# A hybrid encoder layer: two sets of input gates moved into a stage of seven block products ahead of the mLSTM

## The chip, the cores and the metric

The kernel runs on one core of a Trainium2 chip. The metric is the device time of one execution in microseconds (us). Several executions are timed and their median is given; one execution is recorded by the hardware profiler and is the source of every row shown.

## The reference, cut to what matters

One encoder layer is applied to two request groups with shared weights. A group is 512 tokens of 1024 features.

```python
h = rmsnorm(x, g_mix)
u = h @ w_in                       # one input projection, columns split into:
qk, v, o, gates, c_q, c_kv, k_r, gm = split(u)
# (A) bidirectional mLSTM, 4 heads, qk width 128, v width 256
qk = silu(centred_conv(qk, conv_w))                     # 5 taps along the tokens
hm = mlstm_chunkwise(q, k, v, log_i, log_f)             # both directions, added
hm = rmsnorm(hm, g_mhead)                               # per head
y_m = (sigmoid(o) * hm) @ w_mo                          # o: 1024 output gates
# (B) latent attention, 8 heads, latents of 256
y_a = mla_attention(...) @ w_ao
g_m, g_a = split(sigmoid(gm))                           # 2 x 1024 merge gates
x = x + (g_m * y_m + g_a * y_a) @ w_out
x = x + (silu(h2 @ w_gate) * (h2 @ w_up)) @ w_down      # h2 = rmsnorm(x, g_ffn), width 2816
x = x + sigmoid(x @ w_ple_gate) * (p_l @ w_ple)
return rmsnorm(x, g_final)
```

The change concerns `o` (1024 columns), part of `gm` (2048 columns) and the first rmsnorm. Everything is float32.

## The kernel before

**Layout.** Activations lie transposed: 128 features on the partitions, the 512 tokens of one group along the free dimension. The input x of a group is therefore 8 blocks of 128x512 (index `k`), for groups `g` = 0 and 1.

**Split products.** TensorE multiplies in a reduced type (fp32r in the profile). Each float32 operand is split into a high part (a cast on ScalarE) and a low part (a subtraction on VectorE, `lo_of`, L152), and a product is three matmuls: high weight by high row, high by low, low by high. One column block (128 output columns) of the input projection for one group is then 8 blocks x 3 = 24 matmuls of 128x512. This is `proj1` (L181 to L183); its weights are 512 KB, loaded on SyncE's queue and split as `whi`, `wlo` (`weight`, L166 and L152).

**Rows.** The rows that enter the input projection are x times the gain g_mix, split (`split_x`, tiles hh and hl). They are not divided by their root mean square. `norm_x` works out that factor per token, `rs1`, and spreads it over all partitions (ssc: sums over the features; rbc: spreading, by matmuls with a diagonal). `hproj` multiplies each column block by `rs1` on VectorE when it leaves PSUM (L329); for v the factor is a per-partition scale instead (L502, L503).

**mLSTM.** A head stage prepares the gate columns, the latents cq0, cq1, ckv0, ckv1, and the gate logs: the gates go to DRAM (gsd, rid) and come back in another layout (lf), pass through log-sigmoid, cumulative sums and running maxima (L378 to L443) with a trip through DRAM (lfd) for the flipped direction, and end in `nmr`, from which each chain builds its weights. Then `mlstm_proj(hd)` does the projections of a head: q and k with the convolution (VectorE, L477), v (matmuls of 128x256, L495 to L497), the scores sT, and last the two output-gate columns of the head (`to`: L329, then tanh and a scaling by hg, on ScalarE). `mlstm_chain(hd, g)` follows for each group: per direction, bc and bd (matmuls with `nmr`, L543 to L546) give the exponents, ScalarE takes exp into a tile `w` (L558; there is one), VectorE multiplies by the scores, `w` is split into ph and pl (L567, L152), and nm (L580) multiplies by v. The result is normed (ssm, L598), transposed by TensorE (ht, L602), multiplied by `to` and stored (hz). In program order the projections of head hd+1 follow the chains of head hd. Ahead of the chain of (head 3, group 0) stands `lat_norms` (constant `LATN`): it norms the latents with ssc, eight diag, rbc and eight scalings (L620 to L629). Its rbc uses the two PSUM banks (tag bc) that bc and bd use.

**Merge gates.** `merge_gate` does one of the 16 merge-gate columns for both groups by `proj1` (48 matmuls), takes the tanh and stores it to DRAM (tmd, tad). They do not depend on the mLSTM or on attention. The list `BULK` says how many stand where: 10 after the program text of the mLSTM, then 2 and the rest between the attention heads.

**Order.** Each engine works through its own queue in order. The order of the queues comes from a scheduler that simulates the program: it starts from the program's order and lets instructions pass one another where pools of tiles (`Slots`) and PSUM banks (`Banks`) allow it. Merge gates that stand behind the mLSTM in the text therefore run between the last head's matmuls.

**Seven block products.** The output projections of the two branches and the FFN use a scheme with fewer products, the class `Seven` with `Ops` (operands), `chain` (order) and `outputs`: two column blocks, two halves of the contraction and the two groups make a product of 2x2 blocks, which is done by 7 block products (P1, P2, P7, P6, P5, Q4, P3) instead of 8, each 4 x 3 = 12 matmuls (L894 to L896, tile names b, xh, xl, wp). Sums of row blocks (VectorE or GpSimd) and of weight blocks (GpSimd, L869 to L879) are built before; weights of a pair of columns come in 1 MB on ScalarE's DMA queue, and each product's weights are split when they are due.

Of the kernel before, what the change touches and what calls it, by code (L numbers as in the profile page):

```python
# [7 lines left out]
F32 = mybir.dt.float32  # L8
# [54 lines left out]
def encoder_kernel(ctx: ExitStack, tc: tile.TileContext, a):  # L63
# [67 lines left out]

    banks("P1", dict(mm=2, sc=2, tp=2, bc=2), mm="mm", sc="sT nm", tp="ssc tpc vtp ht", bc="bc bd rbc")
# [147 lines left out]

    LAT = Slots("LAT", "right", raw=8)
    H = Slots("H", h=32, rs=2)
    MC = Slots("MC", sel=2)
    X0 = Slots("X0", x=16, raw=2, tr=15)
    R = Slots("R", "right", r=12, tr=2)
    h, rs1 = [], []
    xs = [[X0("x", "x") for _ in range(KD)] for _ in range(G)]
# [16 lines left out]

# [5 lines left out]
    def raw(bk, sl=LAT):  # L310
        t = sl("raw", "raw")
        S.copy(t, bk)
        return t
# [3 lines left out]
    early["gate", 0] = raw(proj1(wg, h[0]), X0)  # L317
# [5 lines left out]
    early["gate", 1] = raw(proj1(wg, h[1]), X0)  # L323
    early["cq0", 1] = raw(proj1(wq, h[1]))
    norm_x(0)
    norm_x(1)

    def hproj(w, g, out, bk=None):
        V.tensor_tensor(out=out, in0=rs1[g], in1=proj1(w, h[g]) if bk is None else bk, op=ALU.mult)  # L329
        return out  # L330
# [14 lines left out]
    for n in ("cq1", "ckv0", "ckv1"):  # L345
        w = w8(n)
        for g in range(G):
            early[n, g] = raw(proj1(w, h[g]))
    X0.close()
# [112 lines left out]
    def mlstm_proj(hd):  # L462
        qk = [[None, None] for _ in range(G)]
        for qi, nme in enumerate(["q", "k"]):
            w = w8(f"{nme}{hd}")
            ch = 4 * qi + hd
            for g in range(G):
                bk = hproj(w, g, M1("tr", "cu"))
# [14 lines left out]
        for g in range(G):  # L483
# [14 lines left out]
            for i in range(NB):  # L498
                src = bks[i // 2][:, 256 * (i % 2) : 256 * (i % 2) + 256]
                hi_, lo_ = (v2[n][:, i, 0:256] for n in range(2))  # L500
                sc = rcol[g][:, 2 * i : 2 * i + 1]
                S.activation(out=hi_, in_=src, func=AF.Copy, scale=sc)  # L502
                V.scalar_tensor_tensor(  # L503
                    out=lo_, in0=src, scalar=sc, in1=hi_.bitcast(F32), op0=ALU.mult, op1=ALU.subtract
                )
# [16 lines left out]
        for c in range(2):  # L522
            w = w8(f"o{2 * hd + c}")
            for g in range(G):
# [114 lines left out]
    tmd = [[dr.tile([P, T], F32, name=f"tmd{g}_{c}") for c in range(KD)] for g in range(G)]  # L639
    tad = [[dr.tile([P, T], F32, name=f"tad{g}_{c}") for c in range(KD)] for g in range(G)]  # L640

    def merge_gate(name, dst, c):
        w = w8(f"{name}{c}")
        for g in range(G):
            t = hproj(w, g, EV("bk", "tg"))
            S.activation(out=t, in_=t, func=AF.Tanh, scale=0.5)
            nc.sync.dma_start(dst[g][c], t)

    bulk = [(n, d, c) for c in range(KD) for n, d in (("gm", tmd), ("ga", tad))]
# [127 lines left out]

    late = {}  # L780
    NAMES = ("P1", "P2", "P7", "P6", "P5", "Q4", "P3")

    def op(name, n, dt):
        return (H if name in ("P1", "P2", "P7", "P6") else late["OP"])("h", n, dt)

    class Ops:

        def __init__(self, raw, tmp, sums):  # L790
            self.raw, self.tmp, self.sums = raw, tmp, sums
            self.r, self.t, self.x = {}, {}, {}

        def get(self, n, k):
            if (n, k) not in self.r:
                self.r[n, k] = self.raw({"a": 0, "b": 1, "c": 0, "d": 1}[n], k + 4 * (n in "cd"))
            return self.r[n, k]

        def part(self, name, k):
            if name in ("P1", "P2", "P3"):  # L800
                return self.get({"P1": "a", "P2": "c", "P3": "d"}[name], k)
            add = self.sums(name).tensor_tensor
            if name == "P7":
                t = self.t[k] = self.tmp() or self.get("b", k)
                add(out=t, in0=self.get("b", k), in1=self.get("d", k), op=ALU.subtract)
            elif name == "P6":
                t = self.t[k]
                add(out=t, in0=t, in1=self.get("a", k), op=ALU.subtract)
            elif name == "P5":
                t = self.get("a", k)  # L810
# [29 lines left out]
    def wsplit(src):  # L840
        n, t = src.shape[-1], wpair()
        hi, lo = t[:, 0:n], t[:, n : 2 * n]
        S.copy(hi, src)  # L843
        lo_of(lo, src, hi)
        return hi, lo

    class Seven:


# [583 lines left out]
```

## Time and profile before

| | |
|---|---|
| median of 3 runs | 1907.61 us (1904.54 to 1908.16) |
| the profiled execution | 1907.19 us |
| its span in the profile | 1905.4 us |
| mean granted TensorE clock | 0.988 |
| TensorE busy | 1849.6 us, 97% |
| VectorE busy | 1242.5 us, 65% |
| ScalarE busy | 879.7 us, 46% |
| GpSimd busy | 477.5 us, 25% |
| DMA | 207.58 MB, mean 109 GB/s |

In the rows, PE is TensorE (PEld its weight loads, beside PE), DVE VectorE, ACT ScalarE, POOL GpSimd, SP SyncE. A row of the time order gives the start, the duration, engine, source line, operation, output <- inputs with their sizes, how many were joined (x8), and in brackets the idle time before with what ended it. Matmuls overlap in the pipeline: a matmul's duration is longer than the distance from its start to the next one's.

### The profile page before, as it was taken

Reading aid. Unit: us, or ns where it says so; the run is one execution under the profiler, and the core shown is the slowest. Engines: PE = TensorE matmul, PEld = TensorE weight load, DVE = VectorE, ACT = ScalarE, POOL = GpSimd, SP = SyncE. Lnnn points to the kernel's source line nnn. Section 1 sums busy time; section 2 is a strip of 40 time slices with the busy share of each in tenths; the row PEclk is TensorE's granted clock in tenths of the full one; section 3 lists DMA queues with packets and bytes.
Section 4 is the critical chain, followed back from the end, with each engine's and each line's share of the span. In section 5 each row is a group of like instructions: output and inputs, shape, how many; then the busy total and the mean of one; then the engine's idle time right before and its main releaser. Section 6 shows DMA issues by size and latency. Waiting matters only on the chain.

```text
span 1905.4 us, 24519 instructions
## 1 busy us (share of the span) xinstructions
PE 1849.6 (97%) x8840; PEld 1538.6 (81%) x8840; DVE 1242.5 (65%) x2141; ACT 879.7 (46%) x1711; POOL 477.5 (25%) x346
## 2 busy tenths in 40 slices
PE   7999999999999999899989998999999999999997
PEld 6898998988888878677877886888888887888886
DVE  7657575836556567976897577444444558878757
ACT  5255555644444565784434354333333344434442
POOL 3000000100000000342550026666465652322100
PEclk9999999999999999999999998999999999999999
DMA  4111111122253123345455241233222346534242
GB/s 164 51 45 34 56 34 56 34 67 73 78 176 132 54 70 110 106 149 210 154 184 181 88 166 50 100 112 109 94 100 93 129 137 222 162 130 141 89 127 89
DMA packets 97881, 207.58 MB, mean 109 GB/s; under 512 B 10656, under 2 KB 21280, under 8 KB 97760
## 3 DMA queue, kind: packets, MB, share of 16 engines
q1 hardware_dynamic: 85664, 163.03, 25.5%
q10 hardware_dynamic: 12096, 43.00, 7.0%
q8 instruction: 69, 1.13, 0.2%
q14 instruction: 52, 0.43, 0.1%
HBM read 151.89 MB, written 54.10 MB: 108 GB/s over the span
## 4 chain that ended last, share of the span: by engine, by line
PE 85%; DVE 8%; issue 2%; ACT 2%; POOL 1%; DMA 1%; SPq 0%; DVEq 0%; ACTq 0%; POOLq 0%
PE b L894 12%; PE b L896 12%; PE b L895 12%; PE mm L183 8%; PE mm L181 8%; PE mm L182 8%; PE nm L580 3%; DVE xl L152 2%; PE mm L79 2%; PE mm L495 2%; PE mm L497 2%; PE mm L496 2%; PE pt L759 1%; DVE wp L152 1%; PE mm L1243 1%
## 5 line engine op out<-in xcount | busy, mean ns | idle before, releaser
L894 PE MATMUL b<-xh,wp 128*128 128x512 f32 x1148 | 444.1, 395 | 13.3 <-ACT wp L843 6.4
L895 PE MATMUL b<-xl,wp 128*128 128x512 f32 x1148 | 451.1, 393 | 4.9 <-DVE xl L152 4.9
L896 PE MATMUL b<-xh,wp 128*128 128x512 f32 x1148 | 447.2, 394 | 3.7 <-DVE wp L152 3.6
L843 ACT CAST wp<-wst 128x512 fp32r<-128x512 f32 (+1 forms) x271 | 164.7, 612 | 306.7 <-PE b L896 238.8
L152 DVE TENSOR_TENSOR wp<-wst,wp 128x512 fp32r<-128x512 f32 (+1 forms) x271 | 248.3, 918 | 76.7 <-ACT wp L843 76.1
L894 PEld LDWEIGHTS b<-xh,wp 128*128 128x128 f32 x1148 | 217.4, 189 | 66.4 <-ACT wp L843 8.8
L896 PEld LDWEIGHTS b<-xh,wp 128*128 128x128 f32 x1148 | 217.4, 189 | 53.5 <-DVE wp L152 6.0
L895 PEld LDWEIGHTS b<-xl,wp 128*128 128x128 f32 x1148 | 217.4, 189 | 52.1 <-DVE xl L152 5.3
L181 PE MATMUL mm<-hh,whi 128*128 128x512 f32 x592 | 233.7, 395 | 7.4 <-ACT whi L166 7.2
L183 PE MATMUL mm<-hh,wlo 128*128 128x512 f32 x592 | 233.1, 396 | 2.3 <-DVE wlo L152 2.2
L182 PE MATMUL mm<-hl,whi 128*128 128x512 f32 x592 | 233.4, 395 | 0.7 <-DVE hl L277 0.7
L869 POOL TENSOR_TENSOR s<-wst,wst 128x512 f32<-128x512 f32 (+1 forms) x42 | 75.6, 1800 | 432.8 <-DMA wst<-w 255.0
L934 DVE TENSOR_TENSOR u<-b,u 128x512 f32<-128x512 f32 x90 | 61.6, 689 | 141.4 <-PE b L896 85.3
L181 PEld LDWEIGHTS mm<-hh,whi 128*128 128x128 f32 x592 | 112.6, 190 | 31.2 <-ACT whi L166 7.2
L183 PEld LDWEIGHTS mm<-hh,wlo 128*128 128x128 f32 x592 | 112.4, 190 | 26.6 <-DVE wlo L152 3.4
L182 PEld LDWEIGHTS mm<-hl,whi 128*128 128x128 f32 x592 | 112.4, 190 | 24.5 <-DVE hl L277 1.3
L166 ACT CAST whi<-wst 128x1024 fp32r<-128x1024 f32 (+1 forms) x71 | 73.0, 1029 | 103.9 <-PE mm L182 63.4
L152 DVE TENSOR_TENSOR xl<-ld,xh 128x512 fp32r<-128x512 f32 x121 | 97.7, 837 | 11.6 <-ACT xh L1178 6.6
L152 DVE TENSOR_TENSOR wlo<-wst,whi 128x1024 fp32r<-128x1024 f32 (+1 forms) x71 | 86.7, 1221 | 25.1 <-ACT whi L166 24.8
L929 ACT COPY u<-b 128x512 f32<-128x512 f32 x90 | 50.9, 588 | 110.6 <-PE b L896 79.1
L152 POOL TENSOR_TENSOR vnl<-avt,vnh 128x512 fp32r<-128x512 f32 x16 | 21.4, 1337 | 283.6 <-ACT vnh L156 260.9
L495 PE MATMUL mm<-whi,hh 128*128 128x256 f32 x256 | 72.3, 283 | 0.2 <-DVE cu L329 0.2
(333 smaller groups left out, 3570.4 us busy)
## 6 DMA issues: line engine op xcount, KB each, us to landing
wst<-w SPq DMA_DIRECT2D x75, 512.0 KB
wst<-w ACTq DMA_DIRECT2D x60, 512.0 KB
ld<-actd SPq DMA_DIRECT2D x77, 256.0 KB
actd<-t SPq DMA_DIRECT2D x44, 256.0 KB
actd<-sg SPq DMA_DIRECT2D x33, 256.0 KB
x<-x SPq DMA_DIRECT2D x32, 256.0 KB
ld<-hzd SPq DMA_DIRECT2D x32, 256.0 KB
wst<-wd ACTq DMA_DIRECT2D x16, 512.0 KB
```

Of the source, the lines that this page charges most:

```text
L152: e.tensor_tensor(out=out, in0=src, in1=hi.bitcast(F32), op=ALU.subtract)
L166: S.copy(hi[:, :n], st[:, :n])
L181: E.matmul(bk, whi[:, c], hi, start=k == 0, stop=False)
L182: E.matmul(bk, whi[:, c], lo, start=False, stop=False)
L183: last_mm[0] = E.matmul(bk, wlo[:, c], hi, start=False, stop=k == nk - 1)
L495: E.matmul(out, hi[:, tb], whi[:, n], start=k == 0, stop=False)
L843: S.copy(hi, src)
L869: GP.tensor_tensor(out=src, in0=a11, in1=a21, op=ALU.add)
L894: E.matmul(bk, whi[:, c], hi, start=bool(first) and k == 0, stop=False, **sk)
L895: E.matmul(bk, whi[:, c], lo, start=False, stop=False, **sk)
L896: E.matmul(bk, wlo[:, c], hi, start=False, stop=k == self.kh - 1, **sk)
L934: V.tensor_tensor(out=t, in0=b, in1=t, op=ALU.add if name == "P2" else ALU.subtract)
```

## The change

1. **Rows are normed once.** `norm_x` no longer squares in place and sums to one block; it squares into tiles of their own, adds them in pairs to four, sums the four by matmuls (four passes of ssc instead of one), spreads the factor with float32 matmuls (`spread_f32`) and multiplies the rows: 8 instructions per group write x * g_mix * rstd over x. `hproj` goes: what leaves PSUM in the mLSTM is copied. The early columns (gate, latents) still use the unnormed rows.
2. **A stage ahead of the mLSTM** makes nine pairs of columns by seven block products of the normed rows: all eight output-gate columns (4 pairs) and the first ten merge-gate columns (`FIRST` = 5 pairs). Both kinds end in tanh (the output gates also in the scaling by hg) and are stored to DRAM (tod, tmd, tad). `mlstm_proj` loads its output gates from tod on SyncE's queue.
3. **The rows of the mLSTM and of later merge gates** are the splits that this stage has made: P1, P2 and P3 of it, and one new split for block b.
4. **What moves with it.** The seven-product code stands earlier in the file. Its pool WX is open from the start; the pools MC and R (the gate logs' tiles) and the PSUM banks P1 are opened behind the stage, so the gate logs come behind it. The latents cq1, ckv0, ckv1 come before the gate logs. `BULK` holds the other 6 merge gates: 2 behind the mLSTM's text, 4 in attention.

Counts: 128x512 matmuls of the plain projection go from 1776 to 912, those of block products from 3444 to 4200. Plain weight loads on SyncE's queue go from 75 to 57, pair loads on ScalarE's from 60 to 78, and SyncE gets 16 loads of output gates. Instructions of VectorE go from 2143 to 2205, of ScalarE from 1701 to 1843, of GpSimd from 351 to 379.

```diff
     def norm_x(g):
-        q = xs[g]
+        q = []
         for k in range(KD):
-            if k in (2, 5):
-                GP.tensor_tensor(out=q[k], in0=q[k], in1=q[k], op=ALU.mult)
-            else:
-                S.activation(out=q[k], in_=q[k], func=AF.Square)
-        for i, j, e in ((2, 5, GP), (0, 1, V), (3, 4, GP), (6, 7, V), (0, 3, V), (2, 6, V), (0, 2, V)):
-            e.tensor_tensor(out=q[i], in0=q[i], in1=q[j], op=ALU.add)
+            t = XT("t", "sq")
+            S.activation(out=t, in_=xs[g][k], func=AF.Square)
+            q.append(t)
+            if k % 2:
+                V.tensor_tensor(out=q[k - 1], in0=q[k - 1], in1=t, op=ALU.add)
+        pc = bank("ssc")
+        sumsq(pc, q[::2])
+        r = rsqrt(pc[:, 0 : 2 * NB], 2 * NB, 1.0 / D)
+        V.tensor_copy(out=rcol[g], in_=r)
+        bc = spread_f32(r)
         t = H("rs", "rs1")
-        S.copy(t, rstd_bank(q[:1], D, X0, rcol[g]))
+        S.copy(t, bc)
         rs1.append(t)
+        for k in range(KD):
+            x = xs[g][k]
+            V.scalar_tensor_tensor(out=x, in0=x, scalar=col("g_mix", k), in1=bc, op0=ALU.mult, op1=ALU.mult)
...
+    hx = Ops(lambda g, k: xs[g][k], lambda: XT("t", "t"), lambda n: V, place0)
+    hx.need("P7")
...
+    def first_pair(*cols_):
+        def put(at, t):
+            (kind, c), g = cols_[at[0]], at[1]
+            o = utile("o") if at == (0, 1) else t
+            S.activation(out=o, in_=t, func=AF.Tanh, scale=0.5)
+            if kind == "o":
+                S.activation(out=o, in_=o, func=AF.Identity, scale=hg[:, c : c + 1], bias=hg[:, c : c + 1])
+            nc.sync.dma_start(dsts[kind][g][c], o)
+
+        srcs = [a["w8"][W8[f"{kind}{c}"]] for kind, c in cols_]
+        return hx, lambda: Seven(srcs, 4, hx, outputs(put, utile))
+
+    banks("PF", dict(b0=2, b1=3, b2=2, sp=1), b0="b0", b1="b1", b2="b2", sp="sp")
+    bulk = [(n, c) for c in range(KD) for n in ("gm", "ga")]
+    quads = [first_pair(("o", 2 * i), ("o", 2 * i + 1)) for i in range(MH)]
+    quads += [first_pair(*bulk[2 * i : 2 * i + 2]) for i in range(FIRST)]
+    bulk = bulk[2 * FIRST :]
+    chain(quads, head=True)
...
+    h = [hx.x["P1"] + hx.x["P2"], bs + hx.x["P3"]]
+    WX.close()
+    XT.close()
+    MC = Slots("MC", sel=2)
+    R = Slots("R", "right", r=12, tr=2)
+    banks("P1", dict(mm=2, sc=2, tp=2, bc=2), mm="mm", sc="sT nm", tp="ssc tpc vtp ht", bc="bc bd rbc")
...
         to = [[None] * 2 for _ in range(G)]
-        for c in range(2):
-            w = w8(f"o{2 * hd + c}")
-            for g in range(G):
-                to[g][c] = hproj(w, g, M1("to", "to"))
-                S.activation(out=to[g][c], in_=to[g][c], func=AF.Tanh, scale=0.5)
-                hc = hg[:, 2 * hd + c : 2 * hd + c + 1]
-                S.activation(out=to[g][c], in_=to[g][c], func=AF.Identity, scale=hc, bias=hc)
+        for g in range(G):
+            for c in range(2):
+                to[g][c] = M1("to", "to")
+                nc.sync.dma_start(to[g][c], tod[g][2 * hd + c])
...
-BULK = [10, 2, 1, 1, 0, 2, 0, 0, 0, 0]
+FIRST = 5
+BULK = [2, 1, 1, 1, 0, 1, 0, 0, 0, 0]
```

The order of TensorE's queue in the last mLSTM head, before: mm (L181 to L183) is a merge gate, nm and bc belong to the chain of the head.

```order
2492 L183 MATMUL mm_5022<-hh_145,wlo_5019 128x512
2493 L181 MATMUL mm_5022<-hh_149,whi_5017 128x512
2494 L580 MATMUL nm_4425<-va_3883,pl_4408 128x258
2495 L580 MATMUL nm_4433<-va_3883,pl_4408 128x258
2496 L580 MATMUL nm_4433<-va_3883,ph_4407 128x258
2497 L580 MATMUL nm_4433<-va_3884,ph_4407 128x258
2498 L580 MATMUL nm_4433<-va_3883,pl_4408 128x258
2499 L182 MATMUL mm_5022<-hl_151,whi_5017 128x512
2500 L183 MATMUL mm_5022<-hh_149,wlo_5019 128x512
2501 L181 MATMUL mm_5022<-hh_153,whi_5017 128x512
2502 L543 MATMUL bc_4599<-nmr,sel_4597 128x512
2503 L182 MATMUL mm_5022<-hl_155,whi_5017 128x512
```

The same place after the change: mm_5885 is the last merge gate that stands here, rbc the spreading of the latents' norms, bc and bd the first of the head's chain.

```order
2806 L181 MATMUL mm_5885<-xh_938,wlo_5854 128x512
2807 L236 MATMUL rbc_5341<-diag_5342,onesr 128x512
2808 L236 MATMUL rbc_5341<-diag_5345,onesr 128x512
2811 L236 MATMUL rbc_5369<-diag_5370,onesr 128x512
2814 L236 MATMUL rbc_5383<-diag_5387,onesr 128x512
2815 L757 MATMUL bc_5398<-nmr,sel_5396 128x512
2816 L759 MATMUL bd_5400<-nmr,sel_5396 128x512
2817 L760 MATMUL bd_5400<-mask_2110,identr 128x512
2818 L757 MATMUL bc_5474<-nmr,sel_5472 128x512
2821 L794 MATMUL nm_5422<-va_5000,ph_5404 128x258
```

The merge gates, which alternated with the chain, are now ahead of it; from row 2807 to the end of the head at row 2954 only the chain's own matmuls follow.

VectorE's queue at the gate logs, before: from the spreading of group 1's factor (diag) over the gates (gsb) to the first steps of the logs (u, lf, z, 128x64).

```order
64 L232 TENSOR_TENSOR diag_412<-ident,rh_407 128x512
65 L232 TENSOR_TENSOR diag_415<-ident,rl_409 128x512
66 L338 TENSOR_TENSOR gsb_432<-raw_286,rs_78_382 128x512
67 L152 TENSOR_TENSOR wlo_564<-wst_560,whi_562 128x1024
68 L378 SCALAR_TENSOR_TENSOR u<-lf 128x64
69 L388 TENSOR_SCALAR lf<-lf 128x64
70 L380 TENSOR_SCALAR z<-u 128x64
71 L381 RECIPROCAL z<-z 128x64
```

After the change, the same steps (u, lf): ahead of them stand the last outputs of the new stage (u from b), the weights of the mLSTM's first projections (wlo) and constants that were made earlier (identr, mask).

```order
206 L150 TENSOR_TENSOR wp_2033<-wst_1862,wp_2033 128x512
207 L150 TENSOR_TENSOR wlo_2268<-wst_2264,whi_2266 128x1024
208 L434 TENSOR_TENSOR u_2028<-b_327_1963,u_2028 128x512
209 L434 TENSOR_TENSOR u_2011<-b_327_1963,u_2011 128x512
210 L574 CAST identr<-ident 128x128
211 L150 TENSOR_TENSOR wlo_2352<-wst_2348,whi_2350 128x1024
212 L586 CAST mask_2110<-mst_2108 128x128
213 L586 CAST mask_2114<-mst_2112 128x128
214 L597 SCALAR_TENSOR_TENSOR u<-lf 128x64
215 L607 TENSOR_SCALAR lf<-lf 128x64
```

The logs have moved from row 68 to row 214, behind the whole stage of block products. At that stage's start, VectorE's queue after the change mixes differences of row blocks (t, x from L305 to L311), low parts of rows (xl) and of weights (wp), and outputs (u):

```order
100 L150 TENSOR_TENSOR xl_719<-t_715,xh_717 128x512
101 L305 TENSOR_TENSOR t_721<-x_106,x_110 128x512
102 L150 TENSOR_TENSOR wp_943<-wst_763,wp_943 128x512
103 L311 TENSOR_TENSOR x_96<-x_96,x_104 128x512
104 L434 TENSOR_TENSOR u_783<-b_168_812,u_783 128x512
105 L150 TENSOR_TENSOR wp_960<-wst_765,wp_960 128x512
106 L308 TENSOR_TENSOR t_715<-t_715,x_97 128x512
107 L150 TENSOR_TENSOR xl_725<-t_721,xh_723 128x512
```

None of these rows has a counterpart before: there the rows were split once, and the products used them as they were.

More of the change, by code (lines that the diff above doesn't have):

```diff
@@ L281, in encoder_kernel @@
     LAT = Slots("LAT", "right", raw=8)
     H = Slots("H", h=32, rs=2)
-    MC = Slots("MC", sel=2)
-    X0 = Slots("X0", x=16, raw=2, tr=15)
-    R = Slots("R", "right", r=12, tr=2)
+    XT = Slots("XT", x=16, t=28)
+    WX = Slots("WX", "right", wst=2, s3=2, wp=1)
+    banks("P0", dict(mm=4, tp=2, bc=2), mm="mm", tp="ssc", bc="rbc")
     h, rs1 = [], []
-    xs = [[X0("x", "x") for _ in range(KD)] for _ in range(G)]
+    xs = [[XT("x", "x") for _ in range(KD)] for _ in range(G)]
     def split_x(g):
```

336 lines of the change are left out of this document (174 added, 162 removed).

## The prediction

> **What bounds the kernel now.** I read the page first (busy shares, the 40 slices), then the same busy times stage by stage, then the time order of the engines at four places.
>
> ```profile
> PE 1849.6 (97%) x8840; PEld 1538.6 (81%) x8840; DVE 1242.5 (65%) x2141; ACT 879.7 (46%) x1711; POOL 477.5 (25%) x346
> PE   7999999999999999899989998999999999999997
> PEclk9999999999999999999999998999999999999999
> ```
>
> TensorE is busy nearly everywhere. The stages tell where it waits (columns: stretch, its length, then busy time and count of PE, PEld, DVE, ACT and POOL, and the granted clock):
>
> ```profile
> 0.00:72.00 72.00, 61.68 (x257) 49.36 (x258) 46.01 (x91) 31.43 (x49) 16.99 (x29) 0.98 0.37 127
> 72.00:431.00 359.00, 358.79 (x2150) 319.12 (x2148) 225.59 (x499) 185.69 (x432) 18.62 (x30) 1.00 0.14 46
> 431.00:540.00 109.00, 109.00 (x546) 92.55 (x546) 65.78 (x166) 47.03 (x116) 1.36 (x2) 1.00 0.25 84
> 540.00:930.00 390.00, 378.47 (x1757) 308.43 (x1756) 270.37 (x506) 230.27 (x447) 71.85 (x52) 0.99 0.39 128
> 1200.00:1550.00 350.00, 348.39 (x1518) 284.22 (x1518) 161.90 (x189) 123.88 (x216) 204.73 (x136) 1.00 0.30 102
> ```
>
> From 72 to 540 us, the mLSTM and its gates, TensorE does not wait at all: a matmul removed there is time saved, and work that stands there covers every latency of the other engines. Busy time counts overlapped matmuls, so a price is a distance between starts. These two rows are 54 matmuls of 128x512 apart: 12.26 us, 0.227 us each.
>
> ```profile
> 50.38 0.39 PE L181 MATMUL mm<-hh,whi 128*128 128x512 f32 x1
> ...
> 62.64 0.39 PE L181 MATMUL mm<-hh,whi 128*128 128x512 f32 x1
> ```
>
> **Removed matmuls.** A pair of gate columns took 2 columns x 2 groups x 8 blocks x 3 = 96; seven block products take 7 x 4 x 3 = 84. Nine pairs (4 of output gates, 5 of merge gates) save 108: 108 x 0.227 = **-24.5 us**, all on the path.
>
> **Rows normed once.** The row sums now run over four partial squares instead of one, and the spread uses four 128x128 f32 matmuls instead of two of 128x512.
>
> ```profile
> 29.45 0.95 PE L219 MATMUL ssc<-onesr,x 128*128 128x2 f32 x8
> 30.26 0.48 PE L182 MATMUL mm<-hl,whi 128*128 128x512 f32 x1
> 1088.13 0.89 PE rbc L244 x8
> 425.50:428.90 3.40, 3.40 (x9) 2.65 (x9) 0.00 (x0) 0.00 (x0) 0.00 (x0) 0.50 0.33 129
> 421.72 2.73 PE L219 MATMUL ssc<-onesr,sq 128*128 128x2 f32 x24
> ```
>
> One group's sum costs 0.81 us (29.45 to 30.26) and will cost four times that: 2 x 2.43 = 4.9. The spread goes from 2 x 0.227 to 0.89: 0.9 for both. After 24 such small matmuls the clock stood at 0.50 for 3.4 us, and 9 matmuls started where 15 fit: 1.4 lost. The second group's sum stands in one run of that length, so I add it once: **+7.2** (5.8 to 8.5).
>
> **Building operands for the products.** New on VectorE: 16 scalings, 16 sums, 28 splits and a weight split per product. From the spread of group 1 to the last operand of the fourth product on the first accumulator, 67 VectorE instructions stand beside 160 matmuls (36.3 us). Alone such an instruction takes 0.62 to 0.69 us, beside a GpSimd sum up to 1.37:
>
> ```profile
> 537.75 2.49 DVE L152 TENSOR_TENSOR ckvl<-raw,ckvh 128x512 fp32r<-128x512 f32 x4
> 1217.57 0.69 DVE L152 TENSOR_TENSOR wp<-wst,wp 128x512 fp32r<-128x512 f32 x1 [1.62 <-ACT wp L843]
> 1230.97 1.29 POOL L870 TENSOR_TENSOR wst<-wst 128x512 f32<-128x512 f32 x1
> 1231.44 1.37 DVE L152 TENSOR_TENSOR wp<-wst,wp 128x512 fp32r<-128x512 f32 x1
> ```
>
> 67 x 0.65 = 43.6, so TensorE waits **+7** (0 if the order leaves slack, 12 if eight weight sums each cost 0.65 more). The Trainium skill ("SBUF — State Buffer", "Who interferes with whom") says that a VectorE instruction with two SBUF inputs and a GpSimd one that reads SBUF exclude each other; the 1.37 row agrees, and by the rule alone the term would be the upper end, 12. I take 7, since most splits start before the sums do. Once running, the products resemble 1200 to 1550 us: 1518 matmuls are 344.6 us of 350, so 756 lose **+2.7** (0.5 to 5). The two first weight pairs, 1 MB, are loaded at once on ScalarE's queue, ahead of x; against that GpSimd no longer squares beside VectorE: 0.
>
> **Entering the mLSTM.** The gate logs moved behind the new stage, since their buffers lie where its weights lay.
>
> ```profile
> 57.48 0.23 DVE L378 SCALAR_TENSOR_TENSOR u<-lf 128x64 f32<-128x64 f32 x1 [4.10 <-DMA lf<-rid]
> 61.92 0.34 SPq L390 DMA_DIRECT2D lfd<-lf  x1
> 67.82 0.41 DVE L400 COPY rf<-rfn 32x512 f32<-32x512 f32 x1 [3.53 <-DMA rfn<-lfd]
> 82.85 0.69 DVE L443 TENSOR_TENSOR nmr<-Mn,nmr 64x512 fp32r<-64x512 f32 x1
> ...
> 111.78 0.28 PE L495 MATMUL mm<-whi,hh 128*128 128x256 f32 x1
> 112.27 0.28 PE L496 MATMUL mm<-whi,hl 128*128 128x256 f32 x1
> ...
> L477 DVE SCALAR_TENSOR_TENSOR cv<-cu,cols,cv 128x510 f32<-128x510 f32 x32 | 24.7, 773 | 3.4 <-ACT cv L471 3.0
> L503 DVE SCALAR_TENSOR_TENSOR va<-mm,rcol,va 128x256 fp32r<-128x256 f32 x32 | 15.4, 481 | 18.4 <-ACT va L502 16.0 <-ACT dn L582 2.2
> ```
>
> Today these 26 us end long before TensorE needs nmr. Now the load of lf stands behind the last outputs on SP's queue (some 5 us: two sums of 0.69, a tanh, four issues and the landing), and 14 convolution steps and 8 other instructions (15 us) stand between VectorE's steps (14 x 0.77 and some 4 for the others), four of them (2.7) in the wait for lfd; two weight splits (2.4) of today's 26 are among the 15. nmr comes 5 + 26 + 15 - 2.7 - 2.4 = 41 us after the last product. q, k and half of v cover 96 x 0.227 + 96 x 0.12 (111.78 and 112.27 are four matmuls apart) + 8 x 0.227 = 35.1, and some of the shortfall comes twice, at the transposes ahead: **+7** (2 to 13).
>
> **Between the heads.** The output gates, 96 matmuls per head, no longer stand between sT and the chain; the first chains still have q and k (21.8 us) ahead. But group 1's v follows the chain of group 0 within 6 matmuls and needs its PSUM bank emptied, two copies and two subtractions of 0.48 us (L503 does today what these will do), in part side by side: 1.3 x 3 heads = **+4** (0 to 10).
>
> **The last head.** Before, ten merge gates stand beside it, now two, and both are through before its first bc.
>
> ```profile
> 431.56 0.38 DVE L620 TENSOR_TENSOR ro<-ssc,rcol 128x8 f32<-128x8 f32 x4 [7.57 <-PE ssc L219]
> L232 DVE TENSOR_TENSOR diag<-ident,rh 128x512 fp32r<-128x512 f32 x4 | 2.7, 686 | 1.3 <-PE rbc L238 1.3
> L629 DVE SCALAR_TENSOR_TENSOR raw<-raw,cols,rbc 128x512 f32<-128x512 f32 x8 | 5.6, 743 | 1.8 <-PE rbc L238 1.8
> L152 DVE TENSOR_TENSOR wlo<-wst,whi 128x1024 fp32r<-128x1024 f32 x2 | 2.4, 1217 | 0.0
> ...
> 455.41 1.66 ACT L558 ACTIVATE w<-bc,mcols 128x128 f32<-128x128 f32 x6 [3.51 <-PE bc L543]
> 459.97 1.27 ACT L567 CAST ph<-w 128x1280 fp32r<-128x1280 f32 x1 [0.99 <-DVE w L566]
> 461.27 1.49 DVE L152 TENSOR_TENSOR pl<-w,ph 128x1280 fp32r<-128x1280 f32 x1 [1.33 <-ACT ph L567]
> 510.17 2.88 PE nm L580 x24
> 526.97 0.17 DVE L196 TENSOR_SCALAR rv<-ssm 128x4 f32<-128x4 f32 x1 [0.64 <-ACT nm L595]
> 529.98 1.14 DVE L598 TENSOR_SCALAR hm<-hm,rw 128x256 f32<-128x256 f32 x4
> 534.66 1.04 PE L602 MATMUL ht<-ident,hm 128*128 128x128 f32 x8
> 535.88 2.17 ACT L156 CAST ckvh<-raw 128x512 fp32r<-128x512 f32 x4
> ```
>
> The latency, from ro: 4.2 to the first diag, as it was before; 8 diags, 8 scalings and a weight split on VectorE, 8 x 0.686 + 8 x 0.743 + 1.2 + 0.5 = 13.1, and only then is a bank free for bc, 0.5. Four units (2 groups x 2 directions) follow one another, for there is one w: 455.41 to 462.76 is 7.35, some 6.6 without the foreign work in it, so 26.4. Then 30 matmuls of the last unit at 0.12 (3.6), denominators and squares 1.9, inverse root 2.4, scaling 1.2, transposes 0.8, and 1.2 for the split of the latents, which starts when ht is through. Sum 55. In it TensorE has 6.8 of the merge gates left, 20 x 0.227 + 120 x 0.12 + 1.6 = 20.5 of its own: 55 - 27.3 = 27.7 idle, and 1.4 for a restart at half clock: **+29**. The ends: 18 with units of 5.5 and a restart at full clock; 35 with units of 7.35 and every nm at half clock. The Trainium skill ("TensorE: Matmul & The Clock Gate", "What's actually happening") has the clock fall to half after one idle window of about 3.4 us. By that rule the chain would run cold throughout, 3.6 longer; the trace agrees in part, since it fell at 425.5 without an idle window.
>
> **Attention** has two merge gates fewer between its blocks. It idles 11.5 of 390 us and its fast stretches need no cover: **+3** (-2 to 8). SP's 16 loads of the stored gates follow stores that end in time, no price.
>
> **Sum.** -24.5 + 7.2 + 7 + 2.7 + 7 + 4 + 29 + 3 = +35.4. The profiled execution took 1907.19 us (span 1905.4), 0.02% under the median of 1907.61: 1942.6, I say **1942**.
>
> **Rivals.**
> (a) It ends faster: VectorE runs ahead of TensorE, so that operands, gate logs and the last head's chain wait for no one. Without these three terms (43 us) the sum is -7.6: 1900. For it: VectorE is idle 40% of 431 to 540. Against: TensorE's order puts both gates ahead of rbc, bc needs a bank that rbc holds, and a chain of 55 us cannot hide behind 27. It decides once the three cost under 4 together, or under 16 with the other terms at their low ends (-20.2).
> (b) VectorE becomes the bound of the new stage: 83 instructions at 1.0 beside GpSimd, against 50 us of matmuls, wait 27 to 33 instead of 7: about 1964. Against: half of the operations have an input in PSUM or precede the sums.
> (c) The heads turn latency-bound without output gates: four units of 7.35 and the tail, 40 us, against 41 of v and chains. It is on the edge; 5 more per head give 1957.
> (d) Gain and losses cancel, with the three terms between these points: 1907.
>
> **How the numbers follow.** My forecast 0.57 (own range 1926 to 1958); (b) 0.14; (c) 0.13; (d) 0.07; (a) 0.09. About 0.2% (3.8 us) is what a measurement can tell from no change: faster 0.09, same 0.07, slower 0.84. With all low ends the sum is -0.2, with all high ends +67. Leaving out (a), (d) and the far part of (b): 1914 to 1963.
>
> **What would show it.** In the profile after: no nm beside mm in the last head, four w groups 6 to 8 us apart, PE some 25 us idle in a stretch of 45, the clock at half there; short waits of the first products for xl; bc waiting for nmr after q and k; b matmuls 0.227 apart otherwise. PE busy without a break between the last tg and the v projection would refute the main term. I am wrong above all if units overlap more than one w allows, or if the new stage waits for VectorE at every product.

## The result, and the profile after

The kernel after takes 1971.71 us (median of 4 runs, 1968.57 to 1976.58) against 1907.88 for the kernel before: ratio 1.034, 95% interval 1.0324 to 1.0357. That is 63.8 us slower, where the prediction said 34 slower, and above its range (1914 to 1963). The profiled execution took 1972.01 us, its span is 1970.2.

From the page of the kernel after: busy times, the 40 slices of TensorE, and its clock by slices.

```profile
PE 1866.2 (95%) x8792; PEld 1543.2 (78%) x8792; DVE 1273.9 (65%) x2203; ACT 933.6 (47%) x1835; POOL 530.8 (27%) x374
PE   8999999989986999899989998999999999999997
PEclk9999999999996999999999999999999999999999
```

48 fewer matmuls are recorded (108 fewer in projections and products, 60 more for the row sums and their spreading), and yet TensorE's busy time is longer: the mean granted clock fell from 0.988 to 0.972, and a matmul of 128x512 that counts as busy for 0.39 us at full clock counts for 0.77 at half (both stand in rows below). The slice with 6 is the last head. Stage by stage, first the kernel after (columns: stretch, length, busy time and count of PE, PEld, DVE, ACT, POOL, granted clock, DMA share, GB/s): the block products, heads 0, 1 and 2 (each from its first sT to the next head's), the last head up to attention's first v matmul, attention.

```profile
79.00:261.00 182.00, 176.95 (x758) 142.04 (x757) 86.53 (x122) 94.16 (x160) 58.32 (x34) 0.99 0.29 100
300.40:384.50 84.10, 83.32 (x569) 76.60 (x568) 52.84 (x123) 50.28 (x135) 3.22 (x9) 1.00 0.13 42
384.50:465.30 80.80, 73.21 (x462) 66.17 (x461) 52.87 (x132) 44.20 (x121) 3.46 (x10) 0.96 0.16 53
465.30:542.80 77.50, 71.83 (x457) 65.61 (x456) 53.12 (x126) 45.65 (x117) 6.63 (x9) 0.96 0.17 55
542.80:633.80 91.00, 67.83 (x319) 54.14 (x317) 53.76 (x165) 41.12 (x113) 1.86 (x3) 0.81 0.16 54
633.80:930.40 296.60, 280.23 (x1296) 225.10 (x1297) 212.19 (x426) 189.87 (x380) 51.35 (x39) 0.97 0.33 107
```

The same stretches of the kernel before, from head 0 on:

```profile
109.70:211.50 101.80, 101.80 (x646) 92.53 (x645) 59.17 (x132) 53.20 (x131) 3.64 (x8) 1.00 0.11 37
211.50:302.80 91.30, 91.30 (x559) 81.98 (x558) 59.92 (x139) 50.77 (x126) 4.42 (x8) 1.00 0.14 47
302.80:393.30 90.50, 90.50 (x555) 81.24 (x554) 60.26 (x133) 51.13 (x122) 7.80 (x10) 1.00 0.14 47
393.30:557.10 163.80, 163.80 (x799) 138.00 (x798) 91.92 (x213) 67.35 (x150) 3.02 (x3) 0.99 0.28 93
557.10:864.20 307.10, 295.57 (x1393) 240.21 (x1392) 207.52 (x421) 195.12 (x384) 52.97 (x39) 0.99 0.33 107
```

Before, TensorE is busy for the whole of every head. After, it is idle in each, above all in the last. To compare stages, I take from each the output gates (96 matmuls a head) and merge gates (48 each) that stand in it, at 0.227 us a matmul. What is left is the same work everywhere, so a difference is waiting or a slow clock:

| stage, us net of gates | before | after | difference | predicted |
|---|---|---|---|---|
| start to the last latent | 72.8 | 79.0 | +6.2 | +7.2 |
| block products beyond 756 x 0.227 | – | 10.3 | +10.3 | +9.7 |
| into the mLSTM, to the first sT | 36.8 | 39.5 | +2.7 | +7 |
| heads 0, 1, 2 | 80.0, 69.5, 68.8 | 84.1, 80.8, 77.5 | +24.1 | +4 |
| last head | 33.0 | 69.2 | +36.2 | +29 |
| attention | 241.8 | 253.1 | +11.3 | +3 |
| after attention | 1041.2 | 1039.8 | -1.4 | 0 |
| 108 matmuls fewer | | | -24.5 | -24.5 |

The differences add to 64.9, the spans differ by 64.8. The first row depends on the run: in the eleven kernels here that share this start it lies between +4.9 and +9.5, and what varies is how much of it ran at half clock. The last head's longest waits (who waited <- for whom: us in all, times, longest):

```profile
PE nm L794 <- ACT nm L809: 5.4, 3, 2.9
PE ht L816 <- DVE hm L812: 4.4, 1, 4.4
PE nm L794 <- ACT hm L803: 3.3, 3, 1.2
PE rbc L236 <- DVE raw L843: 2.8, 2, 1.4
PE bc L757 <- DVE raw L843: 1.7, 1, 1.7
```

The same query on the kernel before (393 to 557 us) names no wait at all. In its place in time, the chain of the four units, the first exp of each, then two of the waits and attention's first matmul:

```profile
585.46 1.66 ACT L772 ACTIVATE w<-bc,mcols 128x128 f32<-128x128 f32 x6 [7.39 <-PE bc L757]
592.20 0.37 ACT L772 ACTIVATE w<-bd,mcols 128x128 f32<-128x128 f32 x1 [1.62 <-DVE pl L150]
598.52 0.37 ACT L772 ACTIVATE w<-bd,mcols 128x128 f32<-128x128 f32 x1 [0.88 <-DVE pl L150]
605.16 0.37 ACT L772 ACTIVATE w<-bd,mcols 128x128 f32<-128x128 f32 x1 [0.88 <-DVE pl L150]
609.69 0.80 PE L794 MATMUL nm<-va,ph 128*128 128x258 f32 x2 [2.95 <-ACT nm L809]
631.16 1.97 PE L816 MATMUL ht<-ident,hm 128*128 128x128 f32 x8 [4.44 <-DVE hm L812]
633.79 0.77 PE L887 MATMUL mm<-whi,ckvh 128*128 128x512 f32 x1 [0.66 <-ACT cqh L154]
```

### The profile page after: what moved, and what is told of

The parts are those of the page before. It is cut to its first block, busy times and chain, and to the rows that moved or that the text cites. A ratio compares the mean times of both kernels' runs of the same rounds, so it can differ in the third digit from the quotient of the medians.

```text
span 1970.2 us, 24776 instructions
## 1 busy us (share of the span) xinstructions
PE 1866.2 (95%) x8792; PEld 1543.2 (78%) x8792; DVE 1273.9 (65%) x2203; ACT 933.6 (47%) x1835; POOL 530.8 (27%) x374
## 4 chain that ended last, share of the span: by engine, by line
PE 53%; DVE 8%; ACT 2%; POOL 2%; issue 1%; DMA 1%; ACTq 0%; SPq 0%; DVEq 0%; POOLq 0%
PE b L394 11%; PE b L396 11%; PE b L395 11%; PE mm L181 2%; PE mm L180 2%; PE mm L179 2%; DVE xl L150 2%; PE mm L79 2%; DVE wp L150 1%; PE mm L1291 1%; PE mm L1292 1%; PE mm L1293 1%; POOL s L369 1%; PE pt L970 1%; PE pj L179 1%
## 5 line engine op out<-in xcount | busy, mean ns | idle before, releaser
L395 PE MATMUL b<-xl,wp 128*128 128x512 f32 x1400 | 550.1, 393 | 7.6 <-DVE xl L150 7.6
L394 PE MATMUL b<-xh,wp 128*128 128x512 f32 x1400 | 541.8, 395 | 15.3 <-ACT wp L343 6.7
L396 PE MATMUL b<-xh,wp 128*128 128x512 f32 x1400 | 546.3, 394 | 3.2 <-DVE wp L150 3.1
L394 PEld LDWEIGHTS b<-xh,wp 128*128 128x128 f32 x1400 | 265.3, 189 | 80.6 <-ACT u L429 11.8
L396 PEld LDWEIGHTS b<-xh,wp 128*128 128x128 f32 x1400 | 265.2, 189 | 63.4 <-DVE wp L150 5.9
L372 POOL TENSOR_TENSOR wst<-wst,wst 128x512 f32<-128x512 f32 (+1 forms) x51 | 89.6, 1758 | 42.1 <-DVE wp L150 38.7
L179 PE MATMUL mm<-xh,whi 128*128 128x512 f32 x224 | 88.0, 393 | 0.2 <-DVE va L150 0.2
L180 PE MATMUL mm<-xl,whi 128*128 128x512 f32 x224 | 87.5, 391 | 0.0
L181 PE MATMUL mm<-xh,wlo 128*128 128x512 f32 x224 | 86.9, 391 | 0.0
L379 POOL TENSOR_TENSOR wst<-wst 128x512 f32<-128x512 f32 (+1 forms) x51 | 69.8, 1369 | 46.3 <-DVE wp L150 44.3
L715 PE MATMUL mm<-whi,xh 128*128 128x256 f32 x256 | 75.2, 294 | 6.4 <-DVE va L150 3.4
L794 PE MATMUL nm<-va,ph 128*128 128x258 f32 x320 | 67.2, 308 | 12.3 <-ACT nm L809 7.2
```

Of the source, the lines that this page charges most:

```text
L179: E.matmul(bk, whi[:, c], hi, start=k == 0, stop=False)
L180: E.matmul(bk, whi[:, c], lo, start=False, stop=False)
L181: last_mm[0] = E.matmul(bk, wlo[:, c], hi, start=False, stop=k == nk - 1)
L372: GP.tensor_tensor(out=a11, in0=a11, in1=a21, op=ALU.add)
L394: E.matmul(bk, whi[:, c], hi, start=bool(first) and k == 0, stop=False, **sk)
L395: E.matmul(bk, whi[:, c], lo, start=False, stop=False, **sk)
```

## The experiments

Theory 1 is place: plain projections that depend on nothing are what TensorE does while a chain's latency runs, and where they are taken away the latency is idle time. Theory 2 is that the new stage itself and what it brings (block products, copies, loads of the stored gates) slows what follows.

**The move alone.** Three kernels start from the kernel before and only move projections ahead of the mLSTM, plain as they were. The first moves eight of the ten merge gates behind the mLSTM:

```diff
+    for _ in range(8):            # behind the latents, ahead of the gate logs
+        merge_gate(*bulk.pop(0))
-BULK = [10, 2, 1, 1, 0, 2, 0, 0, 0, 0]
+BULK = [2, 2, 1, 1, 0, 2, 0, 0, 0, 0]
```

> The kernel before with one edit: eight of its ten merge gates are done by the same plain projections ahead of the mLSTM, so that the last head has two. No matmul is saved or added, no row is normed, no block product. Theory 1 (place): the last head loses as much as in the kernel after, 1907.6 + 36 = 1944. Theory 2: about 1908. My prediction's term for this place (29) would give 1937.

Measured: 1944.66 us, ratio 1.019 (1.0171 to 1.021). Net of gates the last head takes 62.3 instead of 33.0, attention 250.4 instead of 241.8, all else as before. The time is the 1944 of theory 1, but by another sum: the last head lost 29.3 and not 36, and attention 8.7. 29 is what the prediction had for this place; here head 3 still has its output gates. Its last head:

```profile
480.40:586.20 105.80, 88.11 (x414) 72.94 (x413) 59.97 (x169) 48.02 (x122) 2.62 (x3) 0.85 0.15 49
```

The second moves the output gates, stores them and loads them in each head:

```diff
+    for c in range(KD):           # behind the latents
+        w = w8(f"o{c}")
+        for g in range(G):
+            t = hproj(w, g, EV("bk", "to"))
...
+            nc.sync.dma_start(tod[g][c], t)
-                to[g][c] = hproj(w, g, M1("to", "to"))
...
+                nc.sync.dma_start(to[g][c], tod[g][2 * hd + c])
```

> The kernel before with one edit: all eight output-gate columns are done by the same plain projections ahead of the mLSTM, stored in DRAM and loaded in each head, as the kernel after does with them. No matmul saved or added, nothing normed. Theory 1 (place): heads 0 to 2 lose what they lose in the kernel after, 24, the entry 2 and the last head some 3 (its ten gates still cover most): 1907.6 + 29 = 1937. Theory 2 (block products, copies, normed rows slow the heads): 1908 to 1912. My prediction's terms for these places (entry 7, heads 4) give 1919.

Measured: 1936.07, ratio 1.0142 (1.0126 to 1.0157). Heads 0 to 2 net: 88.9, 78.8, 75.5, together 24.9 more than before, and they are idle as in the kernel after (heads 1 and 2):

```profile
286.70:365.50 78.80, 72.68 (x461) 66.13 (x460) 54.90 (x133) 43.21 (x117) 2.70 (x8) 0.96 0.18 54
365.50:441.00 75.50, 70.61 (x455) 64.09 (x454) 55.00 (x133) 44.02 (x112) 6.13 (x10) 0.98 0.18 56
```

The third does both moves:

> The kernel before with the eight merge gates and the eight output-gate columns both done by plain projections ahead of the mLSTM: the places of the kernel after, none of its block products and normed rows. If place is all that costs, heads lose 24, the last head 36, attention 9 to 11, the entry 2: 1907.6 + 73 = 1981. The kernel after then differs from it by -24.5 (108 matmuls fewer), +6 (rows normed) and +10 (starting and feeding the products): 1972. If the losses of the two single moves (36.8 and 28.2 by the two kernels already run) only add, without output gates being missed in the last head too: 1973.

Measured: 1976.2, ratio 1.0371 (1.0355 to 1.0387). Heads +22.6, last head 68.6 (+35.6), attention 251.5 (+9.7). With no block product and no normed row in it, it loses nearly all that the kernel after loses in those places (24.1, 36.2, 11.3). Its last head, to set beside that of the kernel after:

```profile
524.50:614.80 90.30, 67.66 (x318) 53.96 (x317) 55.71 (x167) 41.16 (x114) 1.86 (x3) 0.84 0.15 52
```

The profiled spans (1973.9 and 1970.2) say what the rest of the change is worth: some 4 us gained (6 by the ratios, whose intervals overlap).

**The moves undone.** From the kernel after, the merge gates are put back:

```diff
-FIRST = 5
-BULK = [2, 1, 1, 1, 0, 1, 0, 0, 0, 0]
+FIRST = 0
+BULK = [10, 2, 1, 1, 0, 2, 0, 0, 0, 0]
```

> The kernel after, with all sixteen merge gates done by plain projections again, ten of them behind the mLSTM's text and six in attention as before the change (FIRST = 0); the output gates stay in the stage of block products. Five pairs lose the saving: 60 matmuls x 0.227 = +13.6. Theory 1 (place: plain projections that need nothing were what TensorE did while the chain's latency ran): the last head gives back its 36 us and attention its 11, so 1971.7 + 13.6 - 47 = 1938. Theory 2 (the new stage itself, its stored gates, copies and loads slow what follows): nothing comes back and the time is 1985. Theory 3 (only the last head needs cover, attention's 11 us are a cold clock and chance): 1949.

Measured: 1950.6, ratio 1.0219 (1.02 to 1.0238). The last head is back to 33.2 net, with 1.4 us of waits in it:

```profile
445.10:587.20 142.10, 140.76 (x702) 118.68 (x701) 70.17 (x184) 57.21 (x136) 1.86 (x3) 1.00 0.30 102
```

Attention isn't back, 256.2, so theory 3's number fits best, but its reason accounts for a part at most (see Attention below). Then the output gates are put back into the heads, as plain projections of the normed rows:

```diff
-                to[g][c] = M1("to", "to")
-                nc.sync.dma_start(to[g][c], tod[g][2 * hd + c])
+                S.activation(out=to[g][c], in_=proj1(w, h[g]), func=AF.Tanh, scale=0.5)
...
-    quads = [first_pair(("o", 2 * i), ("o", 2 * i + 1)) for i in range(MH)]
```

> The kernel after, with the output gates done by plain projections inside each head again (on the normed rows), and the ten merge gates left in the stage of block products. Four pairs lose the saving: 48 matmuls x 0.227 = +10.9. Theory 1 (place): heads 0 to 2 give back 22 of their 24 us, the last head is as in the kernel after: 1971.7 + 10.9 - 22 = 1961. Theory 2 (new stage, loads of the stored gates, copies in place of multiplications): at most the loads are gone, 1980 to 1983.

Measured: 1951.69, ratio 1.0226 (1.0211 to 1.0241), 9 better than theory 1's number: heads 82.1, 69.5, 69.2 give back 21.6, and the output gates of head 3 also cover 7.5 of the last head (61.7). Heads 1 and 2 are full again:

```profile
326.30:417.60 91.30, 91.30 (x559) 81.93 (x558) 54.90 (x131) 51.70 (x130) 3.93 (x8) 1.00 0.14 47
417.60:508.60 91.00, 90.85 (x556) 81.39 (x555) 56.51 (x132) 52.77 (x127) 6.54 (x10) 1.00 0.14 47
```

With `BULK = [6, 0, ...]` in the kernel after, attention's four gates go to the last head:

> The kernel after, with the six remaining merge gates all behind the mLSTM's text and none in attention. Theory 1 (place): the last head has 4 more gates, 43.6 us of work, and its idle time falls from 36 to 6 or less; attention has 4 fewer and loses 10 to 20 more than in the kernel after: 1952 to 1962. If only the last head needs cover: 1942. Theory 2: no change, 1972.

Measured: 1955.23, ratio 1.0248 (1.0231 to 1.0265). The last head's net falls from 69.2 to 47.1: 43.6 us of gates fill 22.1. Attention loses 3.7. The time lies in theory 1's range, but by luck: the last head gave back less than the 30 expected, and attention lost less than 10 to 20.

**What the last head's latency is made of.** Two w buffers in the kernel after (`w=1` to `w=2`, `to=4` to `to=2`, `sel=2` to `sel=1`):

> The kernel after with two w buffers in place of one (room for it from two buffers of the loaded output gates in place of four, and one sel in place of two). If the single w spaces the units of the last head, as my prediction has it (units of 7.35), a unit falls to the 5.0 us that ScalarE and VectorE need for it, the last head loses 7 less and heads 1 and 2 some 3 less each: 1958. If w isn't what the units wait for: 1970 to 1972.

Measured: 1964.43, ratio 1.0295 (1.0278 to 1.0312), but not as expected: heads 82.8, 78.9, 74.2 gain 6.5, into the mLSTM 3.3, attention 5, the last head nothing (70.1). Its bc come at 576.2, 578.9, 581.6 and 586.1, so the units start close together, and from the first bc to the last ht it is 47 us as before (576.2 to 623.6; 584.6 to 631.2 in the kernel after). The wait has only moved:

```profile
PE nm L794 <- ACT hm L803: 6.4, 4, 3.0
```

Next, `LATN = (1, 0)` in place of `(3, 0)`, and then both edits:

> The kernel after with the latents' norms at head 1, group 0, in place of head 3, group 0. My prediction puts 18 us of the last head's latency there (inverse root, diag and rbc, scalings, then a bank for bc). If so, the last head idles 14 to 18 less and head 1, which has 96 projection matmuls of head 2 beside it, loses 5 to 10 more: 1959 to 1966. If the norms are hidden behind the two merge gates: 1972 or more.

> Both edits of the two kernels beside it. If w and the norms are separate parts of the latency, the gains add: 1945 to 1952. If the four units of a head wait for something else (the copies out of PSUM, nm's banks), it stays at 1960 or above.

Measured: 1974.81 (ratio 1.0353, 1.0335 to 1.037) and 1965.38 (1.0293, 1.0276 to 1.0309), so moving the norms gains nothing, and with two w no more than two w alone. The norms cost 24.6 in the last head (69.2 to 44.6) and 21.2 in head 1, where they went (80.8 to 102.0): wherever no plain work is left, they are idle time. A bank of nm freed one step earlier:

```diff
-                    S.activation(out=bk[:, 0:256], in_=hm[:, i, :], func=AF.Square, accum_out=ssq[:, i : i + 1])
+                    S.activation(out=sqt, in_=hm[:, i, :], func=AF.Square, accum_out=ssq[:, i : i + 1])
```

> The kernel after with the squares in a chain's second direction written to a scratch tile in place of the PSUM bank of nm, so that a bank is free one ScalarE step earlier (0.6 us). In the last head TensorE waits for that step three times, 5.4 us in all. If the two nm banks pace a unit: last head -3 to -5, heads 1 and 2 some -1 each: 1964 to 1968. If the wait only passes to the next one (the copies by ScalarE): 1971.

Measured: 1964.47, ratio 1.0316 (1.0298 to 1.0335). The time is as expected (though the ratio's interval overlaps that of the kernel after), the place isn't: heads gain 9.6 (82.6, 74.8, 75.4), the last head 1.1. So neither w alone nor that bank alone sets the end of the last head; the two together were not tried. In the kernel after, TensorE, VectorE and ScalarE are busy for 30.0, 29.4 and 27.6 of its 47 us; which sequence of them is the shortest possible stays open. Last, useless matmuls in it:

```diff
+                if hd == MH - 1:
+                    bw = bank("mm")
+                    for n in range(3):
+                        E.matmul(bw, identr, phi[:, 0:T], start=n == 0, stop=n == 2)
```

> The kernel after with 48 useless matmuls of 128x512 in the last head (three after each nm group, of ph by the identity, nothing reads them): 10.9 us of more work. They hold the two mm banks, so that the scheduler also puts the two merge gates beside the chain's end and no longer ahead of it. If the last head's loss is idle time and the half clock, the useless work costs little or nothing: 1968 to 1975, with less half clock. If TensorE were short of time there: 1983.

Measured: 1977.12, ratio 1.0378 (1.036 to 1.0396). That lies between the two expectations, and by the ratios the kernel is slower than the kernel after (1.034). In the profiled run, the fastest of the four, the last head with 10.9 us of useless work and the gates at its end takes 1.4 more than without, at a clock of 0.85 instead of 0.81; what the useless work costs by itself isn't shown, since the gates moved too:

```profile
541.90:634.30 92.40, 76.14 (x367) 59.77 (x366) 53.68 (x165) 38.41 (x109) 1.85 (x3) 0.85 0.14 47
```

**Attention.** The kernel with the merge gates back, with v's stores on ScalarE's DMA queue (`nc.sync` to `S` in one line):

> The kernel with all merge gates back (first experiment) and one more edit: attention's v blocks are stored through ScalarE's DMA queue in place of SyncE's. There TensorE waits 6.3 us for the copies of v, whose tiles wait for stores behind a weight load on SyncE's queue. If that queue is the cause, attention's first unit falls from 51 to 45 and the time from 1950.6 to 1945. If the cause is that gates no longer stand beside the splits of the latents: no change.

Measured: 1949.02, ratio 1.0227 (1.0212 to 1.0243), not to be told from the 1950.6 without it. TensorE's wait there, without and with the edit:

```profile
PE mm L887 <- ACT av L891: 6.6, 2, 6.3
PE mm L887 <- ACT av L891: 4.8, 2, 4.4
```

The queue has some part in that wait, and most of it stays. From the kernel before, with only attention's six gates done ahead of the mLSTM (BULK = [10, 0, ...]):

> The kernel before with the six merge gates that stand in attention done by plain projections ahead of the mLSTM; the ten behind the mLSTM's text stay, so the way into attention is as covered as before. If attention itself needs its gates, it loses 8 to 12 (its loss in the kernel after): 1916 to 1920. If its loss is in the way in (first unit) alone: 1906 to 1910.

Measured: 1915.57, ratio 1.004 (1.0026 to 1.0054). Attention net of gates takes 251.0, 9.2 more, and all else is as before: it does need them, if only for 9 of their 65 us.

**Cover left in place.** Output gates plain in the heads, ten gates plain behind the mLSTM, three pairs ahead (FIRST = 3):

> Every cover of the mLSTM back, block products only where none was taken: output gates plain inside the heads, ten merge gates plain behind the mLSTM, and only the six merge gates of attention by block products ahead (3 pairs). Against the kernel before: -36 matmuls x 0.227 = -8.2, rows normed +6.2, starting and feeding the products +9.5, heads and last head 0, attention as in the kernel beside it (0 to 11): 1915 if attention needs no gates, 1926 if it does. A time below 1905 would say that place is all that stood against the block products.

Measured: 1929.84, ratio 1.0113 (1.0086 to 1.0139). Heads (82.1, 69.5, 69.2) and last head (32.9) are whole. In the profiled run, the slowest of the four, it loses 9.5 to the last latent (3 more than the kernel after in the same code), 9.7 in the block products, 11.2 in attention, 2.4 behind it, and saves 8.2. Place isn't all that stood against the block products: their stage has a fixed price too.

## Why the prediction was wrong

The direction was right, for the last head the mechanism too, and several single terms: 108 matmuls; +6.2 for the rows (+7.2 predicted); 10.3 lost in the block products (9.7), where TensorE waited for xl at the start and then hardly at all (waits that the profile names come to 5.0 of the 10.3):

```profile
95.27 0.51 PE L395 MATMUL b<-xl,wp 128*128 128x512 f32 x1 [2.31 <-DVE xl L150]
PE b L395 <- DVE xl L150: 2.8, 2, 2.3
```

So rival (b), VectorE as the bound of the stage, is out. By the rule of the Trainium skill alone ("SBUF — State Buffer", "Who interferes with whom") the loss there would have been 12 + 2.7; the trace has 10.3. The gate logs ended 38.6 us after the last product, where 41 was worked out, and cost 2.7 instead of 7: the first bc hardly waited.

```profile
298.86 0.68 DVE L662 TENSOR_TENSOR nmr<-Mn,nmr 64x512 fp32r<-64x512 f32 x1
301.79 0.39 PE L757 MATMUL bc<-nmr,sel 128*128 128x512 f32 x1
```

Three terms were too small.

1. **Between the heads**, +4 (0 to 10) predicted, +24.1 measured: 20 of the 29 us that were missed. This is the step that failed. I had written that work standing in the mLSTM covers every latency of the other engines, and then priced what its loss uncovers for the last head alone; for heads 0 to 2 I asked only what the v projection would wait for and took it that q and k cover the rest. Rival (c), heads bound by latency, was the truth. It put 5 on top of the 1.3 per head; measured are 4.0, 11.4 and 8.7, a mean of 8. Even its 1957 is 15 short, since the last head and attention were too small as well. The longest of the waits of heads 1 and 2 (384 to 545 us):

```profile
PE bc L757 <- ACT w L772: 4.6, 1, 4.6
PE mm L715 <- DVE va L150: 3.4, 1, 3.4
PE sT L731 <- ACT st L735: 2.9, 3, 1.1
```

The second is the one predicted. The move of the output gates alone gives 24.9, putting them back returns 21.6: shown.

2. **The last head**, +29 (18 to 35) predicted, +36.2 measured. From ro (569.84) to attention's first v matmul (633.79) it takes 64.0 us, where the sum had 55. Up to the first exp it is 15.6 (17.8 worked out). The units start 6.3 to 6.7 apart (6.6), and the four end after 29.1 (26.4). The term that was mis-sized most is the one behind them: 30 matmuls of the last unit, 3.6. The last pl ended at 614.59, and 57 of the head's 120 nm matmuls still stood behind it; they took 12.1, with waits for ScalarE (nm, hm, above) and in part at half clock:

```profile
613.10 1.49 DVE L150 TENSOR_TENSOR pl<-w,ph 128x1280 fp32r<-128x1280 f32 x1 [0.52 <-ACT ph L781]
626.44 0.28 PE L794 MATMUL nm<-va,pl 128*128 128x258 f32 x1
```

With two w the units start closer and end no sooner, so the reason given for their distance (one w) doesn't set the end. Whether head 3 has its output gates matters only ahead of the first bc: from that bc to attention it takes 49.2 in the kernel after, and 48.5, 48.0 and 49.6 with the merge gates moved, with both moved and with the output gates put back; the last head loses 29.3 and 28.7 where they stand in it, 35.6 and 36.2 where they don't.

The clock was worse than predicted too. I sum up, for matmuls that start at half clock, by how much the distance to the next exceeds the usual one, the median for their size (at most that distance again). That estimate gives 9.1 us in the last head, 1.6 before: 7.5 more, where the prediction had 1.4. The rest of what TensorE lost there went from 0.8 to 29.7, 28.9 more (27.7 predicted). These are two accounts of the same time: the half clock is part of what made the chain longer. Over the whole kernel the estimate goes from 13.9 to 33.6 us, and all else beyond the usual distances from 68.9 to 129.7. The low clock stands in rows like these, of the kernel after (the first and the third are the stretches ahead of two falls; the last one ends at full clock):

```profile
578.30:581.55 3.25, 0.99 (x2) 0.37 (x2) 3.25 (x7) 0.00 (x0) 0.00 (x0) 1.00 0.21 81
581.60:602.00 20.40, 14.35 (x41) 9.73 (x42) 13.33 (x25) 11.60 (x37) 0.58 (x2) 0.50 0.07 26
605.57:608.85 3.28, 1.17 (x10) 0.96 (x9) 2.55 (x7) 2.40 (x11) 0.00 (x0) 1.00 0.00 0
609.00:619.20 10.20, 6.70 (x28) 6.10 (x29) 6.64 (x28) 4.69 (x15) 0.00 (x0) 0.50 0.01 2
602.03:605.44 3.41, 2.33 (x16) 1.84 (x16) 1.91 (x4) 2.34 (x6) 0.00 (x0) 1.00 0.00 0
```

By the rule of the Trainium skill ("TensorE: Matmul & The Clock Gate", "What's actually happening") as the prediction took it, the loss would have been 3.6 higher here, with a chain at half clock throughout. The trace goes with the rule in that the clock fell, and differs twice: it first fell (at 581.55) behind two waits of 1.4 us, with no idle stretch of 3.41 us, and it came back twice within the chain (at 602.0 and 619.1).

3. **Attention**, +3 (-2 to 8) predicted, +11.3 measured. I said that its fast stretches need no cover. They do: six gates taken from the kernel before cost 9.2. The way in also counts: with eight gates gone from the last head but all six in attention, 8.7 is lost. By the estimate above, 3.7 of the 11.3 are half clock. Why the kernel with all gates back, but normed rows, still loses 11 to 14 there isn't settled; neither the stores' queue nor the number of gates explains it. By the same estimate 2.4 to 5.6 of that are half clock.

Rival (a), a gain, needed the operands, the logs and the last head to cost under 4 together; they cost 49 (10.3, 2.7 and 36.2). What would have had to be seen first is simpler than any term: the move alone costs 68 us, and the seven products save 24.5.

No version here beats the kernel before. Where no cover is lost, the stage's fixed price (6.2 for the rows, 10.3 for the products) takes six pairs at 2.7 each to earn back, and the only gates that aren't needed in the mLSTM are attention's three pairs, which attention itself needs (+9.2).

## What to carry to other kernels

Independent work in a stage that shows no idle time is doing two jobs: before moving it, take the stage without it and add up the latencies of every chain that remains, for every repetition and not only for the one where it looks thinnest. A saving in instructions counts only if the instructions saved weren't filling a wait. Where idle time will appear on TensorE, price the clock with it: here, by the estimate above, 61 us of new waiting brought another 20 us lost at half clock.

## What the runs showed of the hardware

The granted clock changes on a grid of 3.41 us: in the last head at 581.55, 602.03, 608.86, 619.10 and 629.34, which is 6, 2, 3 and 3 times 3.41 apart. A stretch need not be idle to count as such: the clock fell to half behind 3.25 us with TensorE busy for 0.99, and at 608.86 behind 3.28 with 1.17, and held behind 3.41 us with 2.33. Once low, it stayed so for 20.5 us in the last head, although TensorE was busy for 14.35 of 20.4.

Nor does the busy time tell when it falls. In the kernel before it fell at 425.51, behind 3.40 us that count as busy throughout, most of its matmuls row sums of 128x2:

```profile
422.10:425.50 3.40, 3.40 (x27) 3.24 (x27) 1.73 (x2) 2.57 (x4) 1.66 (x1) 1.00 0.14 25
```

In the sixteen traces the clock fell 198 times. The busy share of the 3.41 us before a fall goes from 0 to 1.00; counted by the columns that its matmuls stream (an estimate, 0.227 us for 512), none of these stretches was filled to more than 0.47, and of the 8492 stretches at full clock without a fall behind them 100 were filled no more either.

A useless matmul isn't all loss where TensorE waits: with 10.9 us of them, and two gates moved to its end, the last head took 1.4 longer. The kernel as a whole took 5.4 longer (1977.12 against 1971.71), and what part of that they cost isn't shown.
